# The WKV scan of one RWKV layer: both directions through one sequence of small matmuls, on a single core

## Chip, cores and metric

The kernel runs on one core of a Trainium2 chip. The metric is the device time of one execution in microseconds, the median of several runs. The core's engines work from queues of their own, each in order: TensorE (PE, with its weight loads as PEld), VectorE (DVE), ScalarE (ACT), GpSimd (POOL) and SyncE (SP), which issues the DMA transfers.

## What is computed

One batch of 1024 latent tokens and 256 context tokens, 1024 channels, two layers. The first mixes tokens with a bidirectional RWKV-7 scan (16 heads of 64), the second with a Fourier transform; each is followed by a squared-ReLU MLP. The change is in the scan, which the reference writes as a step per token, for each of two directions:

```python
def step(s, inp):
    w_t, k_t, v_t, a_t, b_t = inp[:5]
    sa = jnp.einsum('bhvk,bhk->bhv', s, a_t)
    s = s * w_t[:, :, None, :] + sa[..., None] * b_t[:, :, None, :] + v_t[..., None] * k_t[:, :, None, :]
    y = jnp.einsum('bhvk,bhk->bhv', s, inp[5]) if with_out else None
    return s, y
...
for d in range(N_DIRS):
    rev = d == 1
    yc, s_ctx = _wkv_scan(st_c.get('r'), vh_c, *st_c['dirs'][d], s0, rev)
    yl, _ = _wkv_scan(st_l['r'], vh_l, *st_l['dirs'][d], s_ctx, rev)
```

## The kernel before

**Stages.** The projections come first (about 20 to 640 us of the trace), then the scan (643 to 1335 us), then the readout with the gate and the output projection, the first MLP, the Fourier layer and the second MLP. The projections write the scan's operands to DRAM (`post_k` calls `factor`): `s_bk` holds B and K of each token, multiplied by the inverse decay, `s_ar` the vectors A and R.

**The scan** takes 64 tokens a step, 20 steps (`NCH`), four of context and sixteen of latent tokens; `scan_step(i)` does both directions `d`. Inside a step the recurrence over 64 tokens is a triangular system. With 64 tokens on 64 rows, the first 32 are half z=0 and the last 32 half z=1. The 16 heads are 8 pairs `q` of two heads `hh`, which stand in rows 0-63 and 64-127. The pieces, by the names that this document uses:

- **mms** (L945): B and K times A and R, into four PSUM banks (0-3). ACT copies the B part to `mab` (L954, L958), DVE multiplies the rest with a mask into `L` and `l2` (L961, L966).
- **trs** (L975): transposes of B and K into `bkt`, a copy on ACT (L979).
- **inversion** (`scan_invert`): the 32x32 triangular blocks of both directions are inverted, on DVE (L1094 to L1138, "double" being L1121 to L1124) with two PE pieces, **h** (L1145) and **t** (L1156), into `tt`.
- **decay**: the state `t` that the step before left is multiplied by the decay `pcs`, twice: by DVE straight into the operand `sv` (L1001, one instruction for each `hh`) and by POOL into `st` (L1004), which the readers **yr** and **add** use.
- **x** (L1019): `L` times `sv`, for each direction, into a bank `B`; its four 32x64 results (two halves z, two heads) lie in four groups of 32 columns of the array.
- **u** (L1031): `tt` times the copy of x, for each direction and half; **o** (L1044): half 0 of u, times `mab`, added to half 1 of x. A copy of x is L1026, a copy of u into `sv` L1036, both on ACT. So a direction goes x, copy, u(0), copies, o, copy, u(1), copies.
- **s** (L1056) and **add** (L1062, DVE): the next state. **yr** (L1072) and **y** (L1076): the output, copied by ACT (L1082) and sent by DMA to `s_y`.

In u and o one direction uses two 32x32 tiles of the array at a time, one for each `hh`. fp32 matmuls are recorded twice in the trace, each record with a weight load of its own.

**What sets the order.** All work goes into `Plan`. `plan.add(engine, duration, function, reads, writes, bank)` queues a piece with a duration written by hand; `plan.flex` leaves the engine open. `emit` simulates the engines with these durations, picks by start time and by the longest tail behind a piece, and emits the instructions of every engine in the order found; nothing is reordered on the chip. Where the planner sees PE waiting with a free bank at hand, it puts in **fill** matmuls with the identity (L1814). DMA transfers of the scan stand in SP's queue (L910): operands, `s_y`, and the modulation weights `in_k_mwt_dram` (L885), which DVE multiplies and sums (**mod**, L886) in the steps 3 to 18.

## Time and profile before

| what | value |
|---|---|
| time, median of 3 runs | 3095.93 us (3091.98 to 3108.24) |
| the profiled execution | 3100.86 us, of it 3099.1 us span |
| PE, DVE, ACT, POOL busy in the span | 94%, 61%, 32%, 17% |
| the scan | 643 to 1335 us |
| scan: PE, DVE, ACT busy | 579.5, 472.0, 348.3 of 692 us |
| granted TensorE clock, scan / first MLP | 0.76 / 1.00 |

A row of a line gives its records, the busy time of the line and the mean of one record. Matmuls overlap, so a record's duration is longer than its share of time; the length of a whole burst in the timeline, divided by its records, is the better measure. The clock has two levels, 1.2 and 2.4 GHz; a granted clock of 0.50 is the lower one all the time, 1.00 the higher. "issue" is a wait that no semaphore explains.

### The profile page before, as it was taken

The numbers are of one execution on the slowest core, as the hardware profiler recorded it, in microseconds if no ns is written. First come the engines' busy times: TensorE is split into PE (matmuls) and PEld (weight loads), VectorE is DVE, ScalarE is ACT, GpSimd is POOL, SyncE is SP. The second block draws the span as 40 slices with busy tenths as digits, with TensorE's granted clock in tenths as the row PEclk, the third lists the DMA queues.
The fourth block names the chain that finished last, engine by engine and source line by source line (L and its number), as shares of the span: only waits on it lengthen the run. The fifth ranks groups of instructions, "written<-read, shape, count | busy, mean of one in ns | idle before, by whom it ended". The sixth has DMA issues, their size and how long they took to land.

```text
span 3099.1 us, 65486 instructions
## 1 busy us (share of the span) xinstructions
PE 2905.6 (94%) x27884; PEld 2258.6 (73%) x27884; DVE 1902.2 (61%) x3316; ACT 998.6 (32%) x1943; POOL 535.9 (17%) x449
## 2 busy tenths in 40 slices
PE   9999989988878888799999999999899999999998
PEld 5443446477777777789878888888798788888887
DVE  5397785457666666687566556545877544554456
ACT  4363554245444555443211211111322111111121
POOL 2163452201001000111111001100331110111010
PEclk9999999967777877799999999999989999999999
DMA  9266476623344444553132323211031111111111
GB/s 276 86 182 174 136 194 177 160 66 100 107 128 124 134 117 120 158 186 102 58 109 92 96 89 107 70 48 47 8 120 42 52 47 38 55 48 48 41 45 55
DMA packets 297299, 313.03 MB, mean 101 GB/s; under 512 B 81024, under 2 KB 212224, under 8 KB 297008
## 3 DMA queue, kind: packets, MB, share of 16 engines
q1 hardware_dynamic: 295648, 304.01, 33.1%
q8 instruction: 219, 3.59, 0.5%
q0 software_dynamic: 1360, 4.84, 0.5%
q14 instruction: 72, 0.59, 0.1%
HBM read 246.38 MB, written 62.39 MB: 100 GB/s over the span
## 4 chain that ended last, share of the span: by engine, by line
PE 71%; DVE 10%; DMA 6%; issue 3%; ACT 2%; POOL 0%; SPq 0%; DVEq 0%; ACTq 0%; POOLq 0%
PE ps L364 16%; PE ps L366 16%; PE ps L365 16%; PE ps L617 4%; DMA sW<-in_k_mwt_dram 3%; PE ps L620 3%; PE ps L1031 2%; PE ps L945 2%; PE ps L1056 1%; PE ps L1044 1%; PE ps L1019 1%; PE ps L1072 1%; PE ps L1076 1%; DVE bU L456 1%; PE ps L1156 1%
## 5 line engine op out<-in xcount | busy, mean ns | idle before, releaser
L364 PE MATMUL ps<-rU,rU 128*128 128x512 f32 (+3 forms) x2632 | 979.0, 372 | 9.8 <-DVE rX L1509 8.0
L366 PE MATMUL ps<-rU,rU 128*128 128x512 f32 (+3 forms) x2632 | 974.9, 370 | 6.5 <-DVE rU L1239 3.7
L365 PE MATMUL ps<-rU,rU 128*128 128x512 f32 (+3 forms) x2632 | 974.6, 370 | 0.0
L364 PEld LDWEIGHTS ps<-rU,rU 128*128 128x128 f32 x2632 | 500.5, 190 | 105.1 <-DVE rX L1509 9.1
L366 PEld LDWEIGHTS ps<-rU,rU 128*128 128x128 f32 x2632 | 500.6, 190 | 98.0 <-DVE rU L1239 5.2
L365 PEld LDWEIGHTS ps<-rU,rU 128*128 128x128 f32 x2632 | 500.6, 190 | 89.5
L1509 DVE SCALAR_TENSOR_TENSOR rX<-ps,mods,rX 128x512 f32<-128x512 f32 (+1 forms) x528 | 375.6, 730 | 122.3 <-PE ps L366 120.5
L1239 POOL TENSOR_TENSOR rU<-rW,rU 128x512 fp32r<-128x512 f32 x73 | 117.2, 1611 | 1018.8 <-PE ps L366 521.7
L1488 ACT ACTIVATE rS<-ps 128x512 f32<-128x512 f32 x122 | 73.1, 599 | 680.9 <-PE ps L366 680.2
L620 PE MATMUL ps<-bU,bU 128*128 128x512 f32 (+1 forms) x544 | 237.5, 573 | 2.6 <-ACT bS L423 1.9
L423 ACT CAST rU<-rW 128x512 fp32r<-128x512 f32 x160 | 96.3, 616 | 346.8 <-PE ps L366 251.3
L423 DVE CAST rU<-rW 128x512 fp32r<-128x512 f32 x116 | 56.8, 500 | 221.0 <-PE ps L365 210.1
L423 DVE CAST rU<-rS 128x512 fp32r<-128x512 f32 (+1 forms) x99 | 46.9, 479 | 229.5 <-ACT rS L1491 203.4
L1239 DVE TENSOR_TENSOR rU<-rW,rU 128x512 fp32r<-128x512 f32 x201 | 175.5, 893 | 19.7 <-ACT rU L423 19.3
L620 PEld LDWEIGHTS ps<-bU,bU 128*128 128x128 f32 x544 | 100.2, 193 | 109.1 <-issue 98.2
L617 PE MATMUL ps<-bU,bU 128*128 128x512 f32 x304 | 141.7, 607 | 0.0
L945 PE MATMUL ps<-sU,sX 64*128 64x128 f32 (+1 forms) x1280 | 125.5, 353 | 16.8 <-DVE sU L961 7.8
L945 PEld LDWEIGHTS ps<-sU,sX 64*128 64x128 f32 x1280 | 111.9, 255 | 25.2 <-issue 11.7
L961 DVE TENSOR_TENSOR sU<-ps,sW 64x256 f32<-64x256 f32 x160 | 67.5, 422 | 85.7 <-ACT sX L954 44.8
L1239 POOL TENSOR_TENSOR rU<-rS,rU 128x512 fp32r<-128x512 f32 x39 | 60.7, 1559 | 280.8 <-ACT rU L423 125.9
L1036 ACT COPY sU<-ps 32x512 f32<-32x512 f32 x160 | 92.3, 577 | 43.4 <-PE ps L1031 40.2
L617 PEld LDWEIGHTS ps<-bU,bU 128*128 128x128 f32 x304 | 56.6, 192 | 61.6 <-issue 57.8
(268 smaller groups left out, 3899.2 us busy)
## 6 DMA issues: line engine op xcount, KB each, us to landing
rW<-in_mlp_w_dram SPq DMA_DIRECT2D x256, 256.0 KB
rW<-in_k_mwt_dram SPq DMA_DIRECT2D x96, 256.0 KB
sX<-s_bk SPq DMA_DIRECT2D x40, 512.0 KB
s_ar<-bU SPq DMA_DIRECT2D x32, 512.0 KB
sU<-s_ar SPq DMA_DIRECT2D x64, 256.0 KB
sW<-in_k_mwt_dram SPq DMA_DIRECT2D x64, 256.0 KB
bU<-in_rk_wk_dram SPq DMA_DIRECT2D x48, 256.0 KB
bU<-in_rk_wv_dram SPq DMA_DIRECT2D x48, 256.0 KB
```

The costliest lines, as they stand in the source:

```text
L364: nc.tensor.matmul(out, w[0], x[0], start=start, stop=False)
L365: nc.tensor.matmul(out, w[0], x[1], start=False, stop=False)
L366: nc.tensor.matmul(out, w[1], x[0], start=False, stop=stop)
L423: self.nc.scalar.copy(out, src) if e == "act" else self.engines[e].tensor_copy(out, src)
L617: fn = lambda B=B, x=x, w=w, ms=ms, kt=kt: nc.tensor.matmul(B.tile, x[:, ms], w, start=kt == 0, stop=kt == KT - 1)
L620: fn = lambda B=B, x=x, w=w, ms=ms, kt=kt, n=n: nc.tensor.matmul(B.tile[:, :n], w[:, ms], x[:, :n], start=kt == 0, stop=kt == KT - 1)
L945: nc.tensor.matmul(BB[hh].tile[:, j * P : j * P + nr], bk[HR[hh], q, :], L[hh][HR[hh], q, :nr], start=True, stop=True)
L961: plan.add("dve", 0.41, lambda bv=bv, ro=ro, hh=hh, q4=q4, d=d, L=L: nc.vector.tensor_tensor(L[hh][ro, q4, 0:C], bv()[ro, :, 0:C], self.ma ...
L1036: plan.add("act", 0.58, lambda sv=sv, hh=hh, rows=rows, U=U: nc.scalar.copy(sv[rows[hh], hh].rearrange("p q c -> p (q c)"), U.tile[rows[hh ...
L1239: plan.flex({"dve": n / 960 + 0.07, "pool": n / 440 + 0.08}, lambda e: self.engines[e].tensor_tensor(out(1), src(), f32(out(0)), ALU.subtr ...
L1488: plan.flex({"act": 0.53, "dve": 0.6}, lambda e, B=B, s=s: nc.scalar.activation(s.tile[:, :512], B.tile, AF.Relu) if e == "act" else nc.ve ...
L1509: plan.add("dve", n / 960 + 0.12, lambda B=B, m=m, n=n, xs=xs: nc.vector.scalar_tensor_tensor(xs(), B.tile[:, :n], self.mod(layer, 5, m), ...
```

## The change

- **Lockstep.** x of both directions is written into two shared banks `XB`, one for each half z, instead of one bank for each direction. One copy takes a half of both directions (128 rows). u and o issue both directions in one burst, on four 32x32 tiles (`four`), so that two u, one o and two copies of x stand in a step where there were four, two and four. The copies of u stay eight instructions of 32 rows; the planner may now give them to DVE.
- **Halves swapped.** For that the direction d=1 keeps its two token halves in swapped rows (`RZ`): `factor` writes B with its halves exchanged, and the mask is rolled by 32 rows.
- **Rows of their like.** trs is no longer queued with mms, but in `scan_invert`, direction 0 between h and t and direction 1 behind t; h and t are queued in two halves each. t now writes to the rows that it reads.
- **One decay.** DVE multiplies the whole state once into `st` (L989 of the new kernel), and two copies on ACT or DVE bring it from `st` to `sv`. POOL's instruction goes.
- "double" is queued as four pieces instead of one, with the innermost loops of its sums exchanged. y is queued in two pieces, yr and y. Several durations are other numbers.

```diff
-        self.flex_tt(n, bk[:, :ng, 0], gv(ta), p1[:, :ng], ALU.mult, [kta, kp1], [(kbk, 0)])
+        hv = lambda ap: ap.rearrange("p g (w t) -> p g w t", w=2)
+        self.flex_tt(n, hv(bk[:, :ng, 0])[:, :, flip], hv(gv(ta)), hv(p1[:, :ng]), ALU.mult, [kta, kp1], [(kbk, 0)])
...
+        RZ = [[[slice(hh * 64 + 32 * (d ^ z), hh * 64 + 32 * (d ^ z) + 32) for hh in range(2)] for d in range(2)] for z in range(2)]
...
-                    plan.add(("dve", "dve")[hh], 0.78, lambda rs=rs, hh=hh, d=d, t=t, sv=sv: (nc.vector, nc.vector)[hh].tensor_tensor(
-                        sv[rs, hh], t[rs], self.pcs[rs, d, :, i - 1 : i].broadcast_to([64, 8, C]), ALU.mult),
-                        [kt0, *pcs], [(kv, "s0", hh), (kv, "s1", hh)])
-                plan.add("pool", 1.22, lambda d=d, t=t, st=st: nc.gpsimd.tensor_tensor(
-                    st, t, self.pcs[:, d, :, i - 1 : i].broadcast_to([P, 8, C]), ALU.mult), [kt0, *pcs], [ks])
+                plan.add("dve", 0.76, lambda d=d, t=t, st=st: nc.vector.tensor_tensor(
+                    st, t, self.pcs[:, d, :, i - 1 : i].broadcast_to([P, 8, C]), ALU.mult), [kt0, *pcs], [ks])
+                for hh in range(2):
+                    plan.flex({"act": 0.58, "dve": 0.45}, lambda e, hh=hh, sv=sv, st=st: self.copy_on(e, sv[HR[hh], hh], st[HR[hh]]),
+                              [ks], [(kv, "s0", hh), (kv, "s1", hh)])
...
-            self.at = plan.add("pe", 1.1, x_mm, lall + vall, [(B, 0), (B, 1)], B, load=0.78)
-            for z, rows in enumerate((R0, R1)):
-                half = slice(64 * z, 64 * z + 64)
-                xs, kx = slot("xs")
-                plan.add("act", 0.58, lambda B=B, xs=xs, half=half: nc.scalar.copy(xs[half], B.tile[half]), [(B, z)], [kx], B)
...
-                plan.add("pe", 1.08, u_mm, [kx, kT], [(U, z)], U, load=0.4)
+            self.at = plan.add("pe", 0.6, x_mm, lall + vkeys[d], [(XB[0], d), (XB[1], d)], load=1.0)
+        for z in range(2):
+            xs, kx = slot("xs")
+            plan.flex({"act": 0.58}, lambda e, z=z, xs=xs: self.copy_on(e, xs, XB[z].tile), [(XB[z], 0), (XB[z], 1)], [kx], XB[z])
+            U = self.plan.bank(range(5, 8))
+
+            def u_mm(xs=xs, U=U, z=z):
+                for q in range(8):
+                    for d, hh in four:
+                        rs = RZ[z][d][hh]
+                        nc.tensor.matmul(U.tile[rs, q * C : (q + 1) * C], tt[rs, d * 8 + q, :], xs[rs, q * C : (q + 1) * C],
+                                         start=True, stop=True)
+
+            plan.add("pe", 0.65, u_mm, [kx, kT], [U], U, load=0.25)
...
+        for w in range(2):
+            plan.add("pe", 0.7, lambda w=w: h_mm(w), [kxt, *ms], [(H, w)], load=0.15)
...
+        turned(0)
...
+        for w in range(2):
+            plan.add("pe", 0.75, lambda w=w: t_mm(w), [khp, kxd], [(T, w)], load=0.3)
+        turned(1)
```

The order that the planner makes of it, at two places. On PE in the middle of the scan, around u and o, before (L945 is mms, L1044 o, L1156 t, L1031 u, L975 trs; a row is a matmul with its bank, weights and data, and x its repeats):

```order
2187 L945 MATMUL ps_90<-sU_194,sX_203 128x128
2188 L1044 MATMUL ps_96<-sU_188,sX_202 32x64 x16
2189 L1156 MATMUL ps_94<-sU_175,sU_174 32x32 x64
2190 L1031 MATMUL ps_96<-sU_172,sW_155 32x64 x16
2191 L1031 MATMUL ps_97<-sU_173,sW_155 32x64 x16
2192 L975 MATMUL ps_91<-ident,sX_203 128x64
```

And on PE at such a place with the change (L1034 is o, L1832 fill, L1020 u, L1065 yr):

```order
2436 L1034 MATMUL ps_97<-sU_188,sX_202 32x64
2437 L1034 MATMUL ps_97<-sU_187,sX_202 32x64
2438 L1832 MATMUL ps_96<-ident 128x128 x3
2439 L1020 MATMUL ps_96<-sU_173,sW_155 32x64 x32
2440 L1832 MATMUL ps_95<-ident 128x128 x4
2441 L1065 MATMUL ps_95<-sU_170,sU_193 64x64
2442 L1065 MATMUL ps_95<-sU_170,sU_192 64x64
```

Where o of one direction had t and two u of 16 matmuls behind it, o of both directions now has u of 32 behind it, with fill on either side.

On DVE at the end of a step, before (L1062 is add, L1001 the decay, L1121 to L1124 double, L1135 and L1138 transposes of the inversion, L961 the mask):

```order
1003 L1001 TENSOR_TENSOR sU_187<-sU_171,pcs 64x512 x2
1004 L1121 TENSOR_TENSOR sS_168<-sS_164,sS_165 128x512
1005 L1122 TENSOR_REDUCE sS_160<-sS_168 128x64
1006 L1123 TENSOR_TENSOR sS_168<-sS_165,sS_160 128x512
1007 L1124 TENSOR_REDUCE sS_165<-sS_168 128x8x8
1008 L1062 TENSOR_TENSOR sU_171<-ps_97,sU_170 128x512
1009 L1001 TENSOR_TENSOR sU_189<-sU_171,pcs 64x512 x2
1010 L1135 STREAM_TRANSPOSE sU_175<-sU_174 128x16x32
```

And with the change (L1055 is add, L989 the decay, L1135 and L1089 transposes of the inversion):

```order
997 L1055 TENSOR_TENSOR sU_171<-ps_96,sU_170 128x512
998 L1135 STREAM_TRANSPOSE sU_175<-sU_174 128x512
999 L1055 TENSOR_TENSOR sU_171<-ps_95,sU_170 128x512
1000 L1089 STREAM_TRANSPOSE sS_166<-sX_202 128x512
1001 L989 TENSOR_TENSOR sU_170<-sU_171,pcs 128x512 x2
1002 L1092 SCALAR_TENSOR_TENSOR sS_164<-sS_166,sS_160,sS_164 128x256
```

The two adds, which stood some instructions apart, are next to each other, and the two decays follow both.

Over the whole program, 212 fill matmuls become 330; between the first x and the last y they are 22 and 117. In that stretch the kernel before also has 56 matmuls of the readout (L1332 32, L364 to L366 8 each), the changed one 16 (of L1332's kind).

## Rows read from the trace of the kernel before

**Rows 1.** The page, its head and part 1: busy us, share, instructions.

```profile
span 3099.1 us, 65486 instructions
...
PE 2905.6 (94%) x27884; PEld 2258.6 (73%) x27884; DVE 1902.2 (61%) x3316; ACT 998.6 (32%) x1943; POOL 535.9 (17%) x449
```

**Rows 2.** Busy time by stretch: PE, PEld, DVE, ACT, POOL, then clock, DMA.

```profile
643.00:1335.00 692.00, 579.47 (x16754) 529.28 (x16754) 471.99 (x1030) 348.30 (x741) 70.97 (x68) 0.76 0.41 120
...
1600.00:1800.00 200.00, 200.00 (x864) 161.71 (x862) 119.21 (x226) 38.41 (x64) 21.66 (x14) 1.00 0.32 98
```

**Rows 3.** Groups by line and shape, PE, 643 to 1335 us: busy, mean ns.

```profile
L1031 PE MATMUL ps<-sU,sW 32*32 32x64 f32 x1664 | 70.2, 255 | 7.7 <-ACT sU L1026 3.7 <-issue 3.6
L1044 PE MATMUL ps<-sU,sX 32*32 32x64 f32 x1280 | 63.4, 260 | 9.3 <-ACT sU L1036 7.2 <-issue 1.3 <-ACT sU L1026 0.8
...
L1019 PE MATMUL ps<-sU,sU 128*32 128x64 f32 x2560 | 55.7, 243 | 14.4 <-issue 8.4 <-DMA sU<-s_v 3.3 <-DVE sU L1001 2.6
...
L1031 PE MATMUL ps<-sU,sS 32*32 32x64 f32 x896 | 38.4, 257 | 6.9 <-issue 5.9 <-ACT sU L1026 1.0
...
L1332 PE MATMUL ps<-ident,rS 128*128 128x128 f32 x32 | 5.5, 318 | 0.0
L364 PE MATMUL ps<-rU,rU 128*128 128x256 f32 x8 | 2.9, 368 | 0.0
```

**Rows 4.** Timeline of PE in one step: start, length, burst.

```profile
1005.55 1.92 PE L1031 MATMUL ps<-sU,sW 32*32 32x64 f32 x32
1007.40 1.94 PE L1019 MATMUL ps<-sU,sU 128*32 128x64 f32 x64
1009.26 1.81 PE L945 MATMUL ps<-sU,sX 64*128 64x128 f32 x16
1011.00 1.08 PE L1044 MATMUL ps<-sU,sX 32*32 32x64 f32 x32
...
1031.39 1.27 PE L1156 MATMUL ps<-sU,sU 32*32 32x32 f32 x127
```

**Rows 5.** Windows as in rows 2: the clock around those bursts.

```profile
1004.00:1010.60 6.60, 6.60 (x123) 6.03 (x123) 2.22 (x5) 3.02 (x7) 0.00 (x0) 0.50 0.83 230
1010.80:1020.80 10.00, 8.37 (x328) 7.84 (x325) 7.90 (x21) 7.84 (x19) 0.00 (x0) 1.00 0.20 67
```

**Rows 6.** Timeline of PE: h with a wait inside, fill behind the scan.

```profile
1106.46 1.30 PE L1145 MATMUL ps<-sU,sX 32*32 32x16 f32 x118
1110.74 0.25 PE L1145 MATMUL ps<-sU,sX 32*32 32x16 f32 x5 [2.99 <-issue]
...
1333.64 4.96 PE L1814 MATMUL ps<-ident 128*128 128x128 f32 x42
```

**Rows 7.** Waits of PE, 700 to 1308 us: total, times, longest.

```profile
PE ps L1145 <- issue: 23.6, 12, 3.7
PE ps L1156 <- issue: 14.3, 8, 4.4
...
PE ps L1044 <- ACT sU L1036: 7.0, 10, 2.3
PE ps L1031 <- ACT sU L1026: 4.7, 4, 2.3
```

**Rows 8.** DMA queue of instructions, whole program, then 1096.5 to 1103.6 us: packets, MB.

```profile
q8 instruction: 219, 3.59, 0.5%
...
q8 instruction: 3, 0.05, 2.7%
```

**Rows 9.** Groups as in rows 3, other engines, 643 to 1335 us.

```profile
L1036 ACT COPY sU<-ps 32x512 f32<-32x512 f32 x160 | 92.3, 577 | 43.4 <-PE ps L1031 40.2
L1001 DVE TENSOR_TENSOR sU<-sU,pcs 64x512 f32<-64x512 f32 x76 | 73.9, 972 | 1.8
...
L1004 POOL TENSOR_TENSOR sU<-sU,pcs 128x512 f32<-128x512 f32 x38 | 50.3, 1327 | 229.1 <-DVE sU L1062 105.8 <-PE ps L1072 98.9 <-DVE sS L1123 23.0
...
L1062 DVE TENSOR_TENSOR sU<-ps,sU 128x512 f32<-128x512 f32 x38 | 25.9, 687 | 42.9 <-PE ps L1056 30.5 <-ACT sU L1036 11.6 <-ACT sU L427 0.8
```

More of the change, by code (lines that the diff above doesn't have):

```diff
@@ new lines, in scan_step, with o_mm @@
+            kL = E["kL"]
+            lall = [(kL, "a", 0), (kL, "a", 1)] + [(kL, "k", hh, h4) for hh in range(2) for h4 in range(2)]
+            self.at = plan.add("pe", 0.6, x_mm, lall + vkeys[d], [(XB[0], d), (XB[1], d)], load=1.0)
[10 more added lines that the diff above has]
+            plan.add("pe", 0.65, u_mm, [kx, kT], [U], U, load=0.25)
+            for d, hh in four:
+                rs, sv, kv = RZ[z][d][hh], S[d]["sv"], S[d]["kv"]
+                plan.flex({"act": 0.58, "dve": 0.68}, lambda e, rs=rs, sv=sv, hh=hh, U=U: self.copy_on(
+                    e, sv[rs, hh].rearrange("p q c -> p (q c)"), U.tile[rs]), [U], [(kv, f"s{z}", hh)], U)
+            if z:
+                continue
+            def o_mm():
+                for q in range(8):
+                    for d, hh in four:
+                        nc.tensor.matmul(XB[1].tile[RZ[1][d][hh], q * C : (q + 1) * C], mab[RZ[0][d][hh], 1, d * 8 + q, :],
+                                         S[d]["sv"][RZ[0][d][hh], hh, q, :], start=False, stop=q == 7)
+            plan.add("pe", 0.65, o_mm, [(E["kv"], "s0", hh) for E in S for hh in range(2)] + [
+                (kM, d, hh, h4, 0) for d in range(2) for hh in range(2) for h4 in range(2)], [(XB[1], 0), (XB[1], 1)], XB[1], load=0.25)
@@ L1049, in scan_step @@
+        for d in range(2):
+            E = S[d]
+            L, kL, sv, kv, vall = E["L"], E["kL"], E["sv"], E["kv"], vkeys[d]
             if i < NCH - 1:
@@ L1077, in y_mm @@
                                              start=False, stop=q == 7)
-                plan.add("pe", 2.1, y_mm, vall + [E["ks"], (kL, "a", 0), (kL, "a", 1)]
-                         + [(k2, hh, h4) for hh in range(2) for h4 in range(2)], [Y], Y, load=0.85)
+                plan.add("pe", 0.95, r_mm, vall + [E["ks"], (kL, "a", 0), (kL, "a", 1)], [Y], Y, load=0.5)
+                plan.add("pe", 1.05, y_mm, vall + [(k2, hh, h4) for hh in range(2) for h4 in range(2)], [Y], Y, load=1.0)
                 y, ky = slot("y")
@@ L1108, in four @@
                 nc.vector.tensor_reduce(at(x, 16 * t, [(68, 4), (1, t)]), p, AX.X, ALU.add)
-        plan.add("dve", 1.5, four, [km], [kx, kta])
+        plan.add("dve", 0.9, four, [km], [kx, kta])
         def double(n):
@@ L1140, in scan_invert, with turned, turn, h_mm @@
         H, T = self.plan.bank((4,)), self.plan.bank((4,))
-        def h_mm():
-            for y in range(16):
+        HR = [slice(0, 64), slice(64, 128)]
+        TB = [[self.plan.bank(range(4)) for _ in range(2)] for _ in range(2)]
+        def turned(d):
+            bk, bkt, kt_ = S[d]["bk"], S[d]["bkt"], S[d]["kt"]
+            def turn():
+                for q in range(8):
+                    for hh, rs in enumerate(HR):
+                        nc.tensor.transpose(TB[d][hh].tile[:, q * C : (q + 1) * C], bk[rs, q, :], self.ident[rs, rs])
+            plan.add("pe", 0.85, turn, [S[d]["kb"]], [*TB[d]], load=0.5)
+            for hh, B in enumerate(TB[d]):
+                plan.add("act", 0.68, lambda B=B, hh=hh: nc.scalar.activation(
+                    bkt[:, hh].rearrange("p x t -> p (x t)"), B.tile, AF.Copy, scale=self.sgn[:, hh : hh + 1]),
+                    [B, self.ksgn], [(kt_, hh)], B)
+        def h_mm(w):
+            for y in range(8 * w, 8 * w + 8):
                 for q in Q:
                     nc.tensor.matmul(H.tile[q, y * 16 : y * 16 + 16], mab[q, 0, y, :], xt[q, y, 0:16], start=True, stop=True)
-        plan.add("pe", 3.0, h_mm, [kxt, *ms], [H], H, load=0.15)
+        for w in range(2):
+            plan.add("pe", 0.7, lambda w=w: h_mm(w), [kxt, *ms], [(H, w)], load=0.15)
         hp, khp = slot("hp")
```

91 lines of the change are left out of this document (31 added, 60 removed).

## Prediction

> **What bounds the kernel now.** I read the busy times by stretch first. In the scan PE is busy 579.5 of 692 us at a granted clock of 0.76; in the MLP it is busy all the time at 1.00 [rows 2]. The MLP's matmuls are not touched, so what the change is worth is decided between 643 and 1335 us. There PE has the largest share (84%) ahead of DVE (68%) and ACT (50%), and a step takes 692 / 20 = 34.6 us. The groups by line come next: u and o, the two lines that the change rebuilds, hold 70.2 + 38.4 + 63.4 = 172.0 us [rows 3], 30% of PE's busy time in the stage. Then the waits of PE: little of its idle time is for copies of u and x (7.0 and 4.7 us); more is "issue" ahead of h (23.6 us) and t (14.3 us) [rows 7], which no engine explains. The timeline shows such a wait inside one burst of h: 118 records in 1.30 us, then nothing for 2.99 us, then the rest [rows 6]. PE has 2 x 27884 instructions [rows 1], and the queue that carries instructions moved 219 packets [rows 8]: 255 instructions in each, or 128 matmul records with their loads. At the densest three packets start within 7.1 us [rows 8], so about 3.5 us apart, while t's 127 records take 1.27 us [rows 4]. I take these waits for PE running out of instructions. The scan is thus bound by PE in its order: its bursts, its two clock levels (0.50 and 1.00 in neighbouring stretches [rows 5]), and the supply of its instructions.
>
> **u and o on four tiles.** Before, a step has six bursts of 32 records on two tiles, 120 in the scan; now three of 64 on four tiles, 60 in all. The nearest row is x, which has the same 64 columns of data on four groups of columns: at the lower clock 64 records of x take 1.94 us, 32 of u 1.92 us, in the same stretch [rows 4, 5]; 32 of o take 1.08 us at the higher. Twice the matmuls cost the same time when they use twice the tiles. Over the scan x's 40 bursts take 55.7 us [rows 3], 1.39 us each; 60 of them are 83.6 us, so the term is 83.6 - 172.0 = **-88 us**. The ends: no overlap of the four tiles, 0; and the pace of t (10 ns a record, but with half the columns [rows 4]), 60 x 0.64 = 38 us, -134. I take x, which has the same shape of data.
>
> **Fill.** 95 more fill matmuls stand in the scan, 190 records. 42 records take 4.96 us [rows 6], 0.118 us each: 22 us if all of it delays something, 0 if PE waits there anyway. They stand between o, u and s, just where copies are awaited (next paragraph), so I take **+6**.
>
> **Waits for copies.** While one direction's u was copied, PE could work on the other. Now both wait together. Behind u come four copies of 0.577 us [rows 9]; with two on each of ACT and DVE that is 1.15 us and a few handovers. PE has eight mms in front of o (16 records, 1.81 us at the lower clock [rows 4], about half at the higher), fill and yr in front of s. At the higher clock some 0.5 us a step stays open at one or two places: +10 to +20. The waits that go are 7.0 + 4.7 [rows 7]. I take **0**, ends -12 and +20. Between the steps the path is longer than it was: add, decay (both as L1062's 0.687 us, the same shape [rows 9]) and a copy of 0.58, for two directions in turn at most 3.3 us; PE has yr, h, trs and t in front of x, over 5 us by the paragraph on instructions. Hidden; without that cover it would be 20 x 3.3 = 66 us.
>
> **DVE, ACT, POOL.** DVE loses 76 decays of 0.972 (73.9 us [rows 9]) and gets 38 of about 0.687 (26 us), by the planner's order 38 copies of u (0.577 to 0.687, 22 to 26 us) and 15 of `st` (at most 0.687, 10 us): 11 to 16 us less. POOL loses its 50.3 us [rows 9]; the decays of both engines started together there, which may be why 64 rows took 0.972 us and not 0.687. ACT halves its copies of x, gives away the 38 and gets 61 new ones, all near 0.58 us: -40 x 0.58 - 38 x 0.577 + 61 x 0.58 = -10 us. Neither engine is the bound, and these are 2 to 4% of their busy time: 0. The exchanged loops of "double", the rolled mask and the swapped write of B in the projections move the same number of elements with the same count of instructions: 0.
>
> **Instructions of PE.** In the new order h, trs of both directions, t and x of both stand in a row in most steps: 128 + 64 + 128 + 128 = 448 records, 3.5 packets, 12.3 us at 3.5 us a packet. At the higher clock they need 1.27 + 2.16 (two bursts of 32 at o's pace) + 1.27 + 2 x 1.08 = 6.9 us: 5.4 us of waiting a step, against (23.6 + 14.3) / 17.6 steps = 2.2 before [rows 7]: +3.2 x 20 = +64 us. At the lower clock the row needs about 12 us itself, and nothing is lost. With a clock of 0.76 half of the time is at either level: +32. On the other side "issue" ahead of u and o, 3.6 + 5.9 + 1.3 us [rows 3], should go, since packets catch up while copies are awaited: **+21**, ends 0 and +64.
>
> **Readout.** 56 of its matmuls ran inside the scan's last steps, 16 do now. L364 takes 2.9 us for 8, its two neighbours as much, and half of L1332's 5.5 us goes too [rows 3]: **+11** behind the scan, ends 0 and +14.
>
> **Clock.** Nothing in the rows says that the clock rises or falls with this change. A burst takes 1.08 us at the higher level and 1.92 at the lower, so the lower runs at 0.56 of the higher. At 0.76, 52% of the time is high. PE keeps some 490 us of work; a clock of 0.85 would take 45 us off it, one of 0.68 add 48. I take **0**, with these ends.
>
> **Sum.** -88 + 6 + 0 + 0 + 21 + 11 + 0 = -50 us, on an execution of 3100.9 us: 3051. That execution lies 4.9 us over the median of the runs; against the median it is 3096 - 50 = 3046.
>
> **Rivals.** (1) *The scan settles at a higher clock and its supply of instructions keeps up.* The same matmuls in less time leave fewer idle stretches; the clock gains 45 us and the 21 us of instructions stay away: 3046 - 66 = 2980. For it: at 1600 to 1800 us, with PE always busy, the clock is 1.00 [rows 2]. Against it: PE's busy share falls with this change if only its work shrinks. (2) *The gain is eaten in place.* All 64 us of missing instructions, or a clock of 0.68: 3046 + 43 to 48, so 3089 to 3094, no change. For it: the waits in [rows 6, 7] stand just where bursts are quick, and u and o become quick. (3) *The four tiles don't overlap.* They lie in different groups of rows and write one PSUM bank. Then u and o keep their 172 us, and 3096 + 6 + 21 + 11 = 3134. Against it: t's four tiles do the same, at 10 ns a record, where u on two tiles needs 34 [rows 4]; a quarter to a third, with half the columns, is only possible if they overlap. On this the Trainium skill (TensorEngine Tiling (Array Packing), Restrictions and Gotchas) says that different row tiles cannot access the same PSUM bank at the same time. By that rule this rival would hold; t's row speaks against it. (4) *Slower: the decay waits on DVE.* `st` has one buffer for each direction, and its next writer must wait for the readers, yr among them. On POOL that wait was 98.9 us [rows 9] and blocked nobody; now the masks, which free the banks of mms, and the inversion are queued behind it on DVE. If all of it reached PE: 3046 + 99 = 3145. It turns the result to slower once some 65 of the 99 us arrive. Against it: yr stands right ahead of or behind s of its direction, so DVE would wait one burst longer than for the add anyway; and most of POOL's idle time was for the add itself (105.8 us).
>
> **How the numbers follow.** Forecast 0.50 (3046, own range 3015 to 3080); (1) 0.22; (2) 0.15; (3) 0.05; (4) 0.08. A measurement of this kernel tells 0.5%, 15 us, from no change: faster is below 3080, slower above 3111. Faster: (1) and nearly all of the forecast, 0.70. Same: (2) and the rest of the forecast, 0.18. Slower: (3) and (4), 0.12 after rounding. The range reaches from a little below (1), whose term for u and o could be larger, to the upper end of (2): 2965 to 3105.
>
> **What would show it.** u and o: their three groups fall from 172 us to about 84, and a burst of 64 takes 1.1 or 1.9 us; if it takes twice that, (3) holds. Instructions: the sum of "issue" waits ahead of h, t and x rises from step to step while those ahead of u and o vanish. Clock: the window of the scan at 0.76. Decay: waits of the new decay on DVE for yr, and of mms for the masks behind it. Readout: its matmuls behind the last y. The prediction is wrong if PE's waits for ACT and DVE ahead of o, u, s and x together pass some 50 us, which means that lockstep has no cover, or if the time changes outside the scan.

## Result, and the profile after

The changed kernel takes 3067.0 us (median, 3062.5 to 3070.4), the kernel before 3101.5 us on the same chip: a ratio of **0.9882, 95% interval 0.9866 to 0.9898**, 1.2% or 34 to 37 us faster. An earlier set gave 0.9886 (0.9847 to 0.9925); one of its four executions took 9326.7 us and is left out of that ratio. The forecast was 3046 us, 50 us less than before, so its direction held and its size was some 15 us too large.

The profile is that of the run `again` below, the changed kernel without any edit; the profiled execution (3062.5 us) is the fastest of its set, so differences of spans come out some 5 us larger than the 34.5 us between the medians. Its span, and PE's line of part 1, answer to [rows 1]:

```profile
span 3059.8 us, 65882 instructions
...
PE 2850.6 (93%) x28120; PEld 2200.1 (72%) x28120; DVE 1853.1 (61%) x3324; ACT 991.7 (32%) x1930; POOL 494.5 (16%) x414
```

Three points of the trace divide the span: the first x, the last y, the end. They are read from the lines of x and y, before (L1019, L1076) and after (L1005, L1071); a line gives its count, the shortest, median and longest duration in ns, and the first and last start:

```profile
L1019 PE MATMUL ps<-sU,sU x2560: 216/219/317, 643.2 to 1314.1; 128*32 128x64 f32 x197
L1076 PE MATMUL ps<-sU,sU x1024: 221/222/367, 817.2 to 1333.5; 128*64 128x64 f32 x171
```

```profile
L1005 PE MATMUL ps<-sU,sU x2560: 216/244/317, 645.0 to 1263.3; 128*32 128x64 f32 x197
L1071 PE MATMUL ps<-sU,sU x1024: 216/222/369, 796.9 to 1277.5; 128*64 128x64 f32 x171
```

Up to the first x the two differ by 1.8 us (643.2, 645.0). The scan, first x to last y, falls from 690.3 to 632.5 us: **-57.8**. What follows it grows from 1765.6 to 1782.3: **+16.7**. Together that is -39.3, the difference of the two spans.

The scan by stretch, before and after (columns as in [rows 2]: us, busy time of PE, PEld, DVE, ACT, POOL, granted clock, DMA share, GB/s):

```profile
643.20:1333.50 690.30, 577.77 (x16741) 527.77 (x16740) 470.49 (x1029) 347.51 (x740) 69.82 (x68) 0.76 0.41 120
```

```profile
645.00:1277.50 632.50, 510.86 (x16891) 456.46 (x16890) 409.57 (x1016) 332.62 (x713) 17.11 (x26) 0.83 0.42 125
```

PE is busy 66.9 us less and idle 9.1 us more (112.5 to 121.6), and its granted clock went from 0.76 to 0.83. The groups of PE in the scan answer to [rows 3]:

```profile
L947 PE MATMUL ps<-sU,sX 64*128 64x128 f32 x1024 | 86.8, 314 | 11.0 <-DVE sU L968 5.3 <-ACT sU L423 4.2 <-DMA sX<-s_bk 0.5
L1005 PE MATMUL ps<-sU,sU 128*32 128x64 f32 x2560 | 65.1, 266 | 34.8 <-issue 29.8 <-ACT sU L423 4.9
L1049 PE MATMUL ps<-sU,sU 128*64 128x64 f32 x1216 | 44.9, 229 | 0.4 <-ACT sU L423 0.2 <-DVE sU L423 0.2
L1034 PE MATMUL ps<-sU,sX 32*32 32x64 f32 x1280 | 43.7, 247 | 21.7 <-ACT sU L423 11.9 <-DVE sU L423 4.6 <-issue 4.5
L1071 PE MATMUL ps<-sU,sU 128*64 128x64 f32 x1024 | 41.6, 241 | 1.6 <-issue 1.5
L1832 PE MATMUL ps<-ident 128*128 128x128 f32 x234 | 37.5, 308 | 0.0
L1065 PE MATMUL ps<-sU,sU 64*64 64x64 f32 x1024 | 37.1, 221 | 7.0 <-DVE sU L1055 6.4 <-issue 0.5
L1020 PE MATMUL ps<-sU,sW 32*32 32x64 f32 x1664 | 35.5, 238 | 7.9 <-issue 7.5
...
L1020 PE MATMUL ps<-sU,sS 32*32 32x64 f32 x896 | 20.3, 249 | 2.2 <-issue 2.1
...
L1350 PE MATMUL ps<-ident,rS 128*128 128x128 f32 x16 | 2.1, 276 | 0.0
```

u (L1031 before, L1020 now) fell from 108.6 to 55.8 us, o (L1044, now L1034) from 63.4 to 43.7: 72.5 us less together. Fill (L1832, before L1814) rose from the 7.7 us of 44 records to 37.5 us of 234. x rose from 55.7 to 65.1. mms (L947, 64x128), s (L1049), yr (L1065) and y (L1071), whose matmuls are as many and as large as before, got shorter. Their rows of before:

```profile
L945 PE MATMUL ps<-sU,sX 64*128 64x128 f32 x1024 | 96.4, 344 | 6.6 <-DMA sU<-s_ar 2.7 <-DMA sX<-s_bk 2.4 <-DVE sU L961 0.9
...
L1056 PE MATMUL ps<-sU,sU 128*64 128x64 f32 x1216 | 56.4, 261 | 1.1 <-ACT sU L1036 1.1
...
L1072 PE MATMUL ps<-sU,sU 64*64 64x64 f32 x1024 | 45.6, 251 | 2.5 <-issue 2.5
L1076 PE MATMUL ps<-sU,sU 128*64 128x64 f32 x1024 | 43.3, 248 | 0.0
...
L1814 PE MATMUL ps<-ident 128*128 128x128 f32 x44 | 7.7, 332 | 0.0
```

One step on the timeline shows the new state (start, length, count, and in brackets the wait ahead):

```profile
884.21 1.10 PE L1020 MATMUL ps<-sU,sW 32*32 32x64 f32 x64
...
886.33 0.29 PE L1034 MATMUL ps<-sU,sX 32*32 32x64 f32 x2
886.93 0.29 PE L1034 MATMUL ps<-sU,sX 32*32 32x64 f32 x2 [0.30 <-ACT sU L423]
...
888.13 1.08 PE L1034 MATMUL ps<-sU,sX 32*32 32x64 f32 x58 [0.31 <-ACT sU L423]
```

u's 64 records take 1.10 us; before, 32 of o took 1.08 at the higher clock [rows 4]. o is in pieces: two records when the first copy of u lands, two more 0.6 us later with the next, and so on, and only then the other 58. This is so in most steps: cut wherever the next record starts over 0.2 us later, o's 20 bursts hold 52 short pieces besides their longest ones. The short pieces are 143 of the 1280 records and 17.1 of the 43.7 us; the 20 longest pieces take 26.6 us.

### The profile page after: what moved, and what is told of

Same layout as the page of the kernel before. It is cut to its first block, busy times and chain, and to the rows that moved or that the text cites. A ratio compares the mean times of both kernels' runs of the same rounds, so it can differ in the third digit from the quotient of the medians.

```text
span 9324.6 us, 65882 instructions
## 1 busy us (share of the span) xinstructions
PE 9301.5 (100%) x28120; PEld 5436.8 (58%) x28120; DVE 1810.0 (19%) x3324; ACT 995.4 (11%) x1930; POOL 448.4 (5%) x414
## 3 DMA queue, kind: packets, MB, share of 16 engines
q1 hardware_dynamic: 295648, 304.01, 10.8%
## 4 chain that ended last, share of the span: by engine, by line
PE 100%; ACT 0%; DVE 0%; issue 0%; DMA 0%; DVEq 0%; ACTq 0%
PE ps L365 21%; PE ps L364 21%; PE ps L366 20%; PE ps L620 10%; PE ps L617 6%; PE ps L1832 3%; PE ps L947 3%; PE ps L574 2%; PE ps L770 1%; PE ps L1020 1%; PE ps L1005 1%; PE ps L1049 1%; PE ps L1065 1%; PE ps L1071 1%; PE ps L1172 1%; PE ps L1034 1%
## 5 line engine op out<-in xcount | busy, mean ns | idle before, releaser
L364 PE MATMUL ps<-rU,rU 128*128 128x512 f32 (+3 forms) x2632 | 2628.7, 999 | 1.7 <-ACT rU L423 1.7
L365 PE MATMUL ps<-rU,rU 128*128 128x512 f32 (+3 forms) x2632 | 2623.8, 997 | 0.9 <-DVE rU L1341 0.9
L366 PE MATMUL ps<-rU,rU 128*128 128x512 f32 (+3 forms) x2632 | 2597.7, 987 | 0.0
L365 PEld LDWEIGHTS ps<-rU,rU 128*128 128x128 f32 x2632 | 1244.9, 473 | 779.0 <-issue 776.8
L364 PEld LDWEIGHTS ps<-rU,rU 128*128 128x128 f32 x2632 | 1207.1, 459 | 827.8 <-issue 814.4
L366 PEld LDWEIGHTS ps<-rU,rU 128*128 128x128 f32 x2632 | 1207.7, 459 | 778.7 <-issue 772.3
L620 PE MATMUL ps<-bU,bU 128*128 128x512 f32 (+1 forms) x544 | 843.0, 1788 | 0.0
L620 PEld LDWEIGHTS ps<-bU,bU 128*128 128x128 f32 x544 | 237.3, 451 | 504.9 <-issue 498.2
L617 PE MATMUL ps<-bU,bU 128*128 128x512 f32 x304 | 511.0, 1931 | 0.0
L617 PEld LDWEIGHTS ps<-bU,bU 128*128 128x128 f32 x304 | 129.9, 435 | 299.2 <-issue 292.3
L1832 PE MATMUL ps<-ident 128*128 128x128 f32 x660 | 283.7, 628 | 2.7 <-DMA ident<-in_k_ident_dram 2.7
L1832 PEld LDWEIGHTS ps<-ident 128*128 128x128 f32 x660 | 268.1, 577 | 21.7 <-issue 18.2
L947 PE MATMUL ps<-sU,sX 64*128 64x128 f32 (+1 forms) x1280 | 275.8, 578 | 1.3 <-ACT bW L423 1.3
L947 PEld LDWEIGHTS ps<-sU,sX 64*128 64x128 f32 x1280 | 258.4, 568 | 19.8 <-issue 17.8
L620 PE MATMUL ps<-bW,bU 128*128 128x512 f32 (+1 forms) x96 | 141.5, 1640 | 0.0
```

What stands on the lines that cost most here:

```text
L364: nc.tensor.matmul(out, w[0], x[0], start=start, stop=False)
L365: nc.tensor.matmul(out, w[0], x[1], start=False, stop=False)
L366: nc.tensor.matmul(out, w[1], x[0], start=False, stop=stop)
L617: fn = lambda B=B, x=x, w=w, ms=ms, kt=kt: nc.tensor.matmul(B.tile, x[:, ms], w, start=kt == 0, stop=kt == KT - 1)
L620: fn = lambda B=B, x=x, w=w, ms=ms, kt=kt, n=n: nc.tensor.matmul(B.tile[:, :n], w[:, ms], x[:, :n], start=kt == 0, stop=kt == KT - 1)
L947: nc.tensor.matmul(BB[hh].tile[:, j * P : j * P + nr], bk[HR[hh], q, :], L[hh][HR[hh], q, :nr], start=True, stop=True)
```

## Experiments

Each kernel below is the changed kernel with one edit, unless it says otherwise. Ratios are to the kernel before on the same chip, in runs taken together with it; kernels that were not run together are compared by their ratios. "Scan" and "behind" are measured as above; a table of them stands at the end of this section.

**again**: no edit.

> The changed kernel itself, once more, for a profile of an undisturbed execution. Time as measured for it: 3059 to 3070 us. By the prediction's terms the scan shrinks by about 60 us less 11 us of readout moved behind it; with 29 us gained instead of 50, about 20 us must show as one of: more 'issue' waits ahead of h, t, x than the 53 us estimated for the stage, a lower granted clock than 0.76 in the scan, or waits for copies and for DVE ahead of o, u, s and x above 20 us.

Measured 3067.0 us, ratio 0.9882 (0.9866 to 0.9898). It is what the others are held against.

**two_tiles**: u and o keep everything of the change but issue one direction behind the other, so two tiles work at a time in place of four.

```diff
-                for q in range(8):
-                    for d, hh in four:
+                for d, q, hh in [(d, q, hh) for d in range(2) for q in range(8) for hh in range(2)]:
```

> The changed kernel with u and o issuing first direction 0 and then direction 1, so that two tiles work at a time as before the change; all else and the order of all pieces is the same. Theory A (the four tiles overlap and their time stands in the path): u and o take about 88 us more, the time rises to about 3067 + 60 to 88, that is 3127 to 3155. Rival (their time is covered by waits for copies or for instructions): the time rises by under 30 us, to below 3097. Rival (the four tiles do not overlap): no change.

Measured 3121.6 us (3115.4 to 3123.3), ratio 1.0055 (1.0039 to 1.0072): 54.6 us slower than `again`, between the ranges of theory A and its first rival and nearer to A, and 0.55% slower than the kernel before. Its scan by stretch, its groups of u and o, and a burst:

```profile
644.60:1333.80 689.20, 585.67 (x16889) 536.84 (x16890) 410.29 (x1017) 333.05 (x713) 18.05 (x27) 0.79 0.39 116
```

```profile
L1019 PE MATMUL ps<-sU,sW 32*32 32x64 f32 x1664 | 60.9, 250 | 4.0 <-issue 3.9
L1032 PE MATMUL ps<-sU,sX 32*32 32x64 f32 x1280 | 57.9, 272 | 16.4 <-ACT sU L423 10.6 <-issue 2.8 <-DVE sU L423 2.4
...
L1019 PE MATMUL ps<-sU,sS 32*32 32x64 f32 x896 | 36.2, 264 | 2.5 <-issue 2.5
```

```profile
939.16 1.79 PE L1019 MATMUL ps<-sU,sW 32*32 32x64 f32 x64
```

u and o take 155.0 us here and 99.5 in `again`, 55.5 more; the scan is 56.7 us longer. A burst of 64 takes 1.79 us at the higher clock, with four tiles 1.10. That the two differences agree is chance: over the whole scan PE is busy 74.8 us more than in `again` (585.7 for 510.9) and idle 18.1 us less. So the use of four tiles, with all that follows from it, is worth 55 us, and the rest of the change by itself does not speed the kernel up: this scan (689.2 us) is as long as that of the kernel before (690.3), and what is behind it 13.6 us longer. In the same instructions, only reordered, the clock of the scan is 0.79 in place of 0.83: the quicker bursts came with a higher clock, not a lower one.

**old_decay**: the decay as it was, two multiplications of 64 rows on DVE and one on POOL for each direction.

```diff
-                plan.add("dve", 0.76, lambda d=d, t=t, st=st: nc.vector.tensor_tensor(
-                    st, t, self.pcs[:, d, :, i - 1 : i].broadcast_to([P, 8, C]), ALU.mult), [kt0, *pcs], [ks])
                 for hh in range(2):
...
+                    plan.add("dve", 0.78, lambda rs=rs, hh=hh, d=d, t=t, sv=sv: nc.vector.tensor_tensor(
+                        sv[rs, hh], t[rs], self.pcs[rs, d, :, i - 1 : i].broadcast_to([64, 8, C]), ALU.mult),
+                        [kt0, *pcs], [(kv, "s0", hh), (kv, "s1", hh)])
+                plan.add("pool", 1.22, lambda d=d, t=t, st=st: nc.gpsimd.tensor_tensor(
```

> The changed kernel with the decay as before: twice 64 rows on DVE straight into the operand and once on POOL into st, no copies from st. By the prediction the new decay neither gains nor costs: 3060 to 3075. Rival (the decay's wait on DVE for the readers of st, and the longer path through a copy, cost what is missing): 3067 minus 20, about 3045. Rival (POOL beside DVE slows both, and its removal is part of the gain): 3067 plus 15 to 40.

Measured 3071.1 us (3068.2 to 3073.3), ratio 0.9893 (0.9876 to 0.9909), 4 us over `again`, inside both intervals, so in time the new decay neither gained nor cost anything that these runs can tell. Its one profile divides otherwise than that of `again`: the scan is 27.3 us longer (659.8), what is behind it 8.1 us shorter and the start 7.5 us earlier, and x waits 9.2 us for the decay on DVE, where in `again` it waits 4.9 us for the copies on ACT. What the new decay does inside the scan is therefore not settled. The wait that was feared on DVE is not there; its group in the changed kernel was idle for 0.1 us ahead of 38 decays:

```profile
L989 DVE TENSOR_TENSOR sU<-sU,pcs 128x512 f32<-128x512 f32 x38 | 24.8, 673 | 0.1
```

**h_twice**: each matmul of h split into two of 8 columns, 128 records and as many weight loads more in each step for the same work.

```diff
-                    nc.tensor.matmul(H.tile[q, y * 16 : y * 16 + 16], mab[q, 0, y, :], xt[q, y, 0:16], start=True, stop=True)
+                    nc.tensor.matmul(H.tile[q, y * 16 : y * 16 + 8], mab[q, 0, y, :], xt[q, y, 0:8], start=True, stop=True)
+                for q in Q:
+                    nc.tensor.matmul(H.tile[q, y * 16 + 8 : y * 16 + 16], mab[q, 0, y, :], xt[q, y, 8:16], start=True, stop=True)
```

> The changed kernel with each matmul of h split in two of 8 columns: 128 records and 128 loads more in a step, nothing else moved. Theory (PE runs out of instructions: one packet of 255 instructions more in a step, 3.5 us each): up to 20 x 3.5 = 70 us more, about 3110 to 3137, with 'issue' waits grown by 40 us or more. Rival (the waits named issue are not the supply): only the time of the matmuls themselves, 128 x 10 ns x 20 = 26 us more, 3085 to 3095.

Measured 3141.3 us (3138.3 to 3147.7), ratio 1.0125 (1.0108 to 1.0142): 74 us over `again` and just above the range of the theory. PE's waits in the scan (total, times, longest), first here and then in `again`:

```profile
PE ps L1161 <- issue: 34.9, 21, 3.8
PE ps L1005 <- issue: 27.1, 16, 3.9
PE ps L1020 <- issue: 14.7, 11, 2.5
```

```profile
PE ps L1005 <- issue: 29.8, 17, 3.0
PE ps L1172 <- issue: 17.2, 12, 3.1
PE ps L1034 <- ACT sU L423: 11.9, 35, 1.0
PE ps L1020 <- issue: 9.6, 8, 2.2
PE ps L1159 <- issue: 9.4, 10, 1.6
...
PE ps L1034 <- issue: 4.5, 4, 1.7
```

The queue of instructions over the scan, h_twice and `again`, and their groups of h:

```profile
q8 instruction: 152, 2.49, 1.4%
```

```profile
q8 instruction: 132, 2.16, 1.4%
```

```profile
L1161 PE MATMUL ps<-sU,sX 32*32 32x8 f32 x2560 | 61.9, 183 | 34.9 <-issue 34.9
L1159 PE MATMUL ps<-sU,sX 32*32 32x8 f32 x2560 | 61.2, 183 | 15.3 <-issue 13.0 <-DVE sU L1135 2.4
```

```profile
L1159 PE MATMUL ps<-sU,sX 32*32 32x16 f32 x2560 | 31.0, 184 | 11.5 <-issue 9.4 <-DVE sU L1135 2.0
```

(The two lines of h_twice run through each other in one burst, so their busy times cover the same time.) 20 packets more, as 2 x 2560 instructions are, and all waits for issue go from 73.8 to 106.0 us, 32 more, where the theory wanted 40 or more. h's own bursts double from 31.0 us to about 62, since 8 columns take as long a record as 16. Both come with the number of instructions; 3.5 us of waiting for each packet, which the supply theory allowed at most, is not what is seen: 32 us for 20 packets are 1.6 us each. The other 22 us of the 85 by which the scan is longer are mostly busy time of other bursts, at a granted clock of 0.78 in place of 0.83; what lowered the clock is not shown.

**no_fill**: no filling matmuls in the steps of the scan.

```diff
-                for _ in range(op["fills"][0]):
+                for _ in range(0 if op["step"] is not None and op["step"] < 19 else op["fills"][0]):
```

> The changed kernel without the filling matmuls in the scan's 16 steps (234 of them, 37.5 us of TensorE there after the change; they write into banks that are not read). All else is issued in the same order. Theory of the prediction: a fill stands in a gap that exists anyway and overlaps little with other work, so they cost +6 us against before; without them the scan's gain is 0 to 6 us larger (3061 to 3067 against 3067). Rival: 37.5 us of fill stand in a step that is bound by TensorE, so taking them out gives 15 to 37 us (3030 to 3052). Second rival: the fills are what raised the granted clock of the scan from 0.76 to 0.83; without them it falls back to about 0.76 and the time goes up by 10 to 40 us (3077 to 3107).

Measured 3057.6 us (3055.4 to 3058.5), ratio 0.9876 (0.9851 to 0.9900), against 0.9882 for the changed kernel: no difference that the ratios can tell. Its scan by stretch:

```profile
637.00:1274.90 637.90, 492.83 (x16679) 440.45 (x16678) 409.60 (x1015) 331.81 (x713) 17.88 (x27) 0.82 0.41 125
```

The scan is 5.4 us longer than `again`'s, at a clock of 0.82; 32.0 of the 37.5 us of fill are gone, PE's busy time fell by 18.0 us and its idle time rose by 23.4. So the fill stands in gaps that are there without it, and it does not hold the clock up. It also hides waits: without it PE waits 32.6 us for ACT and DVE ahead of o, u, s and x, where it was 21.8 in `again` and 16.4 before the change.

**before_gated** and **after_gated**: in the kernel before and in the changed kernel, each of the readout's loads of y waits for the last step's y, so that no readout runs beside the scan.

```diff
-            ys = [[("sy", d, 2 * t + z) for z in range(2)] for d in range(2)]
+            ys = [[("sy", d, 2 * t + z) for z in range(2)] + [("sy", 0, 15), ("sy", 1, 0), ("sy", 1, 8)] for d in range(2)]
```

(In the kernel before, the two added keys are those of blocks 0 and 15 of each direction.)

> The kernel before, with every load of y of the readout (also those of token blocks whose two directions are done earlier) waiting for the last step's two y: the readout can no longer begin beside the scan, as is the case after the change. Nothing is left out. Theory: this is what the 16.6 us are that the changed kernel is longer behind the scan, so this kernel is 11 to 17 us slower than before (3107 to 3118 against 3096 to 3101) while its scan from the first x to the last y stays at 690 us or gets up to 6 us shorter. Rival: the readout's head start is worth nothing, since what waits behind the scan are loads and planner choices that the change moved otherwise: 0 to 3 us.

> The changed kernel with the same edit: every load of y of the readout waits for both directions' last y. Theory: the halves swapped in one direction put all pairs of y at the end already, so next to nothing is left of the overlap and this costs 0 to 6 us (3067 to 3073). Rival: the readout still runs beside the last steps for as much as before, and the gate costs the same 11 to 17 us as it does the kernel before (3078 to 3084).

Measured: before_gated 3122.4 us, ratio 1.0096 (1.0064 to 1.0128); after_gated 3091.0 us, ratio 0.9977 (0.9959 to 0.9995). The first turn of the readout, in the kernel before, in before_gated, in `again` and in after_gated:

```profile
L1332 PE MATMUL ps<-ident,rS x128: 270/273/476, 1307.9 to 1450.2; 128*128 128x128 f32 x128
```

```profile
L1332 PE MATMUL ps<-ident,rS x128: 270/273/476, 1332.8 to 1469.1; 128*128 128x128 f32 x128
```

```profile
L1350 PE MATMUL ps<-ident,rS x128: 270/273/421, 1270.3 to 1409.2; 128*128 128x128 f32 x128
```

```profile
L1350 PE MATMUL ps<-ident,rS x128: 270/273/477, 1305.6 to 1443.9; 128*128 128x128 f32 x128
```

Without a head start the first turn comes 20 to 22 us behind the last y in both (last y at 1312.8 and 1283.6), and what is behind the scan is nearly equal: 1806.0 and 1810.3 us. With it, the turn comes 25.6 us ahead of the last y in the kernel before and 7.2 us ahead in the changed one. So the theory is right that most of the 16.7 us behind the scan come from the later readout: with both gates 4.3 us of them are left. But its price for the whole is another matter. Both kernels lose about the same by the gate, 1.0096 and 0.9977 / 0.9882 = 1.0096 in ratio, 25 to 30 us. In the kernel before the gate also takes 25.5 us off the scan (690.3 to 664.8): the readout had been paid for there. Both expectations fell, and their rivals' sizes too: the head start of the changed kernel is worth as much as that of the kernel before.

**supply_plan, plan_x, plan_gated, plan_no_fill, old_lengths**: the planner is told other lengths for h, t and x, which changes the order that the planner finds. What is computed stays, but the choices left to the planner move too: in supply_plan DVE makes 78 of the copies of u and `st` in the scan where it made 53 in `again`, and the whole program has 562 records of fill in place of 660. The change had cut those lengths: h from 3.0 us to two halves of 0.7, t from 1.9 to two of 0.75, x from 1.1 a direction to 0.6.

```diff
-            self.at = plan.add("pe", 0.6, x_mm, lall + vkeys[d], [(XB[0], d), (XB[1], d)], load=1.0)
+            self.at = plan.add("pe", 1.2, x_mm, lall + vkeys[d], [(XB[0], d), (XB[1], d)], load=1.0)
...
-            plan.add("pe", 0.7, lambda w=w: h_mm(w), [kxt, *ms], [(H, w)], load=0.15)
+            plan.add("pe", 1.4, lambda w=w: h_mm(w), [kxt, *ms], [(H, w)], load=0.15)
...
-            plan.add("pe", 0.75, lambda w=w: t_mm(w), [khp, kxd], [(T, w)], load=0.3)
+            plan.add("pe", 1.5, lambda w=w: t_mm(w), [khp, kxd], [(T, w)], load=0.3)
```

plan_x has the first of the three edits alone, plan_gated adds the gate above, plan_no_fill adds the edit of no_fill, and old_lengths is no_fill with the lengths of the kernel before (h 1.5 and t 0.95 a half, x 1.1).

> The changed kernel with other planned durations for the three runs of the smallest matmuls: x 1.2 us a direction for 0.6, h 1.4 us a half for 0.7, t 1.5 us a half for 0.75. It changes the order of the work on TensorE alone (t and x then stand apart from each other or side by side in other places), not the work. Theory of the instruction supply (72.8 us of waits for issue in the scan): an order in which a run of small matmuls is followed by long ones lowers them; here 10 to 30 us of them go if the runs come apart (3037 to 3057), and the time goes up if they come together. Rival: the waits are independent of the order, since the number of instructions is the same: within 6 us of 3067.

> The changed kernel with one planned duration put back near what it was before the change: x 1.2 us a direction for 0.6; h and t keep the shorter ones. Theory: the gain of supply_plan hangs on all three runs being costed at what they take, so x alone gives a part of it, 3045 to 3060. Rivals: x alone gives it all (3032 to 3038), or nothing (3061 to 3073).

> The order of supply_plan with the readout's loads of y held back until the last step's two y, as in after_gated (3091). Theory: the 32 us of supply_plan come from its readout work standing earlier beside the last steps (its first turn is 28 us ahead of the last y, for 7 us in the changed kernel) and from 9 us in the scan; held back, only the 9 us are left and it comes out at 3080 to 3086. Rival: the order of h, t and x itself shortens the steps by most of the 32 us, and it comes out at 3055 to 3068.

> Both edits at once: the planned durations of supply_plan (3035) and no filling matmuls in the steps of the scan (10 us less by itself). Theory: the two gains are apart, one in the order of the work in and behind the scan, the other ahead of the first x, so they add up: 3022 to 3028. Rival: the fills stand in gaps that the other order has closed already, so nothing more is won: 3032 to 3038.

> The changed kernel without fills in the scan, and with the planned lengths that h, t and x had before the change: h 1.5 us a half (3.0 whole), t 0.95 a half (1.9 whole), x 1.1 a direction; no other edit. Theory: what plan_no_fill (3023) won over no_fill (3058) is that these three are no longer planned as short, whatever the exact figures; then this one comes out within 10 us of it (3013 to 3033). Rival: such an order is a matter of chance, and small differences in the planned lengths lead anywhere between the two or above: 3035 to 3060. The waits for issue in the scan are expected between 70 and 95 us either way, since plan_gated had 93 and the changed kernel 73.

Measured: supply_plan 3034.6 us, ratio 0.9805 (0.9779 to 0.9831); plan_x 3051.2, 0.9839 (0.9822 to 0.9856); plan_gated 3063.2, 0.9884 (0.9864 to 0.9903); **plan_no_fill 3023.3, 0.9756 (0.9740 to 0.9772)**, the fastest of all; old_lengths 3044.6, 0.9835 (0.9800 to 0.9870). The scan of plan_no_fill by stretch, and its group of o:

```profile
636.20:1245.10 608.90, 473.90 (x16691) 427.57 (x16690) 438.69 (x1062) 320.40 (x694) 23.68 (x32) 0.83 0.46 137
```

```profile
L1034 PE MATMUL ps<-sU,sX 32*32 32x64 f32 x1280 | 35.1, 239 | 13.1 <-DVE sU L423 5.9 <-issue 3.6 <-ACT sU L423 3.1
```

plan_x and plan_no_fill came out as their theories said; in plan_gated and old_lengths the rival did, and supply_plan is below its range. The reason that led to the edit did not hold: waits for issue in the scan did not fall, they are 94.6 us in supply_plan, 79.3 in plan_no_fill and 81.7 in old_lengths, against 73.8 in `again`. What fell are o's waits for the copies (16.5 us in `again`, 9.0 in plan_no_fill) and o's own time (43.7 to 35.1): more work stands between u and o, in one step two bursts of mms in 2.06 us where `again` has one of 1.16, and o has 29 short pieces of 9.7 us in place of 52 of 17.1. But u now waits 9.7 us for the copy of x, which it did not in `again`, where fill stands in that gap (7.7 us in no_fill):

```profile
PE ps L1020 <- ACT sU L423: 9.7, 11, 1.8
```

plan_gated is 0.0093 under after_gated, so the planner's other order, without any head start of the readout, is worth 28 us. Fills off is worth 0.0049 with this order, where it was worth nothing with the other. And old_lengths, whose lengths differ from those of plan_no_fill by 0.1 us for h and x and by 0.55 us for t, is 21 us slower: these differences were enough for another order and another time. Why one order beats the other by 20 us is not settled beyond o's share.

| kernel | ratio | first x | scan | behind | waits for issue in the scan |
|---|---|---|---|---|---|
| before | 1 | 643.2 | 690.3 | 1765.6 | 61.5 |
| before_gated | 1.0096 | 648.0 | 664.8 | 1806.0 | 70.3 |
| again | 0.9882 | 645.0 | 632.5 | 1782.3 | 73.8 |
| two_tiles | 1.0055 | 644.6 | 689.2 | 1779.2 | 65.6 |
| old_decay | 0.9893 | 637.5 | 659.8 | 1774.2 | 86.4 |
| h_twice | 1.0125 | 636.5 | 717.7 | 1781.2 | 106.0 |
| no_fill | 0.9876 | 637.0 | 637.9 | 1780.3 | 80.2 |
| after_gated | 0.9977 | 644.6 | 639.0 | 1810.3 | 82.9 |
| supply_plan | 0.9805 | 644.9 | 623.8 | 1769.0 | 94.6 |
| plan_x | 0.9839 | 640.3 | 638.3 | 1769.4 | 73.8 |
| plan_gated | 0.9884 | 641.8 | 621.5 | 1805.9 | 93.4 |
| plan_no_fill | 0.9756 | 636.2 | 608.9 | 1770.3 | 79.3 |
| old_lengths | 0.9835 | 643.1 | 624.9 | 1773.8 | 81.7 |

(us, from one profile each; the start differs by up to 12 us between profiles, though PE's matmuls are the same up to there.)

## Why the prediction was right, and where its sizes were off

**u on four tiles.** Right to a microsecond: 40 bursts by x's 1.39 us are 55.6 us, and u takes 55.8; 17 of its bursts took 1.09 or 1.10 us, as 18 of x's 40 did before. The rival in which tiles that write one PSUM bank do not overlap is refuted: 64 records take 1.10 us where two_tiles needs 1.79. The rule of the Trainium skill that it rested on (TensorEngine Tiling (Array Packing), Restrictions and Gotchas) is not borne out as a limit on time by these rows.

**o on four tiles.** This is the term that was mis-sized. 20 bursts by 1.39 us are 27.8 us, and o takes 43.7: 19.7 us gained where 35.6 were forecast. The step at fault is the price by x's burst, which is whole, while o's is broken by the copies that it reads. I had put those copies down as waits, at nothing on balance, and as waits they stayed small: 21.8 us ahead of o, u, s and x, below the 50 that I had named as the sign of a failure. But a burst that starts with its first copy and is held for each of the others also gets longer by its pieces, and that is busy time in this view: the longest pieces of the 20 bursts take 26.6 us, what the forecast allowed for all of o, and the 52 short ones 17.1 us on top. In plan_no_fill, with more work between u and o, it is 25.4 and 9.7 us. The missing 15.9 us are about the difference between the forecast (-50) and the result (-35), but that is chance, as the sum below shows.

**Fill.** Forecast +6 with an end at 0; 190 records more came, as forecast, and their price is nothing measurable (no_fill). Had I taken the end, the sum would have been 6 us further off.

**Waits for copies.** Forecast 0, and in `again` PE's waits for ACT and DVE ahead of o, u, s and x rose by 5.4 us (16.4 to 21.8). That is so because fill stands in the gaps; without it they rose by 16.2 us, inside the term's ends but not 0. So this term was too low, and part of lockstep's waits shows as fill.

**Waits for issue.** Forecast +21, measured +12.3 (61.5 to 73.8). The place was half right: ahead of x they grew from 8.4 to 29.8 us, ahead of t from 14.3 to 17.2, but ahead of h they fell from 23.8 to 9.4. Those ahead of u and o did not vanish; they went from 10.8 to 14.1.

**Readout.** Forecast +11, and 11.3 us of its matmuls left the scan: 5.5 + 2.9 + 2.5 + 2.5 us before, 2.1 now. Behind the scan it is 16.7 us. The step's error was to add this without taking it off the scan, where the same matmuls had been in the way: the net in the two profiles is 5.4 us, and with both kernels gated the change is worth as much (1.0096 to 0.9977) as without the gates, so the net cost is near 0.

**Clock.** Forecast 0 at 0.76; it rose to 0.83. Four groups whose matmuls stayed as they were take 31.3 us less, mms, s, yr and y (241.7 to 210.4 in all); in two_tiles, at 0.79, they take 226.7. How much of this is the clock and how much their new places in the order is not separated. x, on the other hand, takes 9.4 us more: 18 of its 40 bursts took 1.10 us or less before, 3 do now. I had argued that a smaller share of busy time on PE speaks against a higher clock; PE is in fact busy 0.81 of the scan now, for 0.84 before, and the clock is higher all the same. Why it rose is not shown; two_tiles shows that the part from 0.79 to 0.83 went with the use of four tiles. This was rival 1's half; its other half, that the supply keeps up, did not come.

**Decay.** The wait for yr on DVE did not come: 0.1 us, and old_decay shows no difference in time.

**DVE.** Decays and copies take 16.6 us less (73.9 to 24.8 + 26.2 + 6.3), where 11 to 16 were forecast. The exchanged loops of "double", put at nothing because the elements are as many, were worth time on DVE: its second multiplication of 128x512 takes 726 ns where it took 1091, and 705 in old_decay, where POOL has its decay back. All multiplications of that line (L1123, now L1120) took 32.6 us in the scan and take 23.0 now.

In sum: the forecast's own mechanism carried the result (two_tiles), and that the total came within some 15 us is in part luck. Of the -39.3 us of the spans, against -50, u and o gained 15.5 us less than forecast, and fill holds 23.8 us more of busy time than its term, in gaps that are there without it. The lines of PE also overlap 11.7 us less than before, and the start is 1.8 us later. The other way went PE's idle time, 9.1 us more where 21 were forecast, the readout, 5.4 us net for 11, and the lines that kept their matmuls (mms, s, yr, y, h, t, trs and x), 24.6 us less where nothing was forecast.

## What to carry to other kernels

A burst priced by another burst of the same shape is right only when its inputs are all there at its start: count the copies that it reads (here four, and 17 us of short pieces), and look whether the order leaves time for all of them between the producer and the burst. Filler in a gap makes a wait look like work: take it out before calling the waits small. When work moves from one stage to another, it comes off the first as it is added to the second, unless a row shows that it ran in a gap. In a kernel whose order a planner sets, its planned lengths are part of the change: here other lengths gave 13 to 37 us by the ratios (plan_x against the changed kernel, plan_no_fill against no_fill), up to as much as the change itself, and the gain could not be read from the lengths themselves.
